# Six buffers of split weights placed at six different addresses modulo 512 bytes

## The chip, the cores and the metric

The kernel runs on one core of one Trainium2 chip. The metric is the device time of one execution in microseconds (us), the median of several runs. Before the change it is 2036.37 us, the median of 3 runs that lie between 2035.35 and 2038.08 us.

## The reference

One decoder layer on 256 tokens with a model width of 2048, all in float32. Cut to what matters:

```python
h = rmsnorm(x, attn_norm_w)
z, xbc, dt_raw, q, k, v, g = split(h @ w_in)          # 2048 -> 20544 columns
y_ssm  = ssd_mixer(z, xbc, dt_raw, ...) @ w_ssm_out    # 4096 -> 2048
y_attn = moba_attention(q, k, v, ...) @ w_attn_out     # 2048 -> 2048
g_ssm, g_attn = split(sigmoid(g + b_gate))
x = x + (g_ssm * y_ssm + g_attn * y_attn) @ w_out      # 2048 -> 2048
h = rmsnorm(x, ffn_norm_w)
u = causal_dwconv(h @ w_up, ffn_conv_w, ffn_conv_b)    # 2048 -> 11264
x = x + (silu(u_gate) * u_up) @ w_down                 # 5632 -> 2048
```

Nearly all arithmetic is in these seven products of a weight matrix with 256 tokens. The attention and the state-space mixer between them are small.

## The kernel before, in words

**Split products.** Every large product is made three times in the fast float32 form ("fp32r") to keep accuracy. A weight w is split into a rounded part `whi` and a remainder `wlo`, the activations likewise into a high and a low part, and a result is the sum of whi·high, whi·low and wlo·high, gathered in one PSUM tile named `mm`.

**The stream of weights.** `unit` (L167) loads 128 x 2048 floats of weights, 1 MB, from HBM into `wraw` (three buffers) by a DMA on SyncE's queue, and makes two chunks of it, c = 0 and 1. For each chunk ScalarE copies 1024 columns into `whi` (L181) and VectorE subtracts to make `wlo` (L182). There are three buffers of `whi` and three of `wlo`, 128 x 1024 floats or 4096 bytes in a partition each, used in turn. So ScalarE can fill a buffer when TensorE has finished the chunk three before.

**Two forms of product.** They differ in which operand sits in the array (the stationary operand, put there by a LDWEIGHTS instruction that the profile counts as PEld) and which is streamed past it (the moving operand).

- `cm_chunk` (L191): the *weights are stationary* and the activations move. For each of 8 blocks of 128 weights of a chunk it issues two matmuls with the same `whi` block (L196 with the high part, L197 with the low part of the activations), then 8 with the blocks of `wlo` (L199). Each moves 256 columns. A chunk is 24 matmuls. This form makes the whole of the kernel from the gates on (about 300 us to the end). The activations are called `hp`, `ot`, `hn`, `yt`, `mt`, `fh` and `a` in turn.
- `tm_chunk` (L340): the *weights move*, 512 columns at a time, and the activations `hp` are stationary (L347 and L348 with `whi`, L353 with `wlo`). This form makes v, q and k, in the first 300 us or so. A chunk is 12 matmuls.

`dt_unit` (L603) uses `whi` alone for a small product, once.

**What sets the order.** The order in which each engine gets its instructions is that of the program text. Steps of the attention and of the mixer are put between units of the weight stream by a small helper (`Spread`). Small matmuls of these steps stand in TensorE's stream between two units: transposes with an identity in `small` (L443, L487 to L489, L701), scores and values of the attention (L209 to L211, operands `kh`, `kl`, `qh`, `ql`, `pth`, `ptl`, `vt`), the mixer's outputs (L752 with 512 columns and L753 with 256, moving `mhl`, stationary `xx`) and a sum over partitions (L264, moving `nsp`, stationary `onesr`).

**Where things lie.** Pools give out SBUF in the order of the program text, and small unused tiles (`pad0` to `pad5`) shift what comes after them. The start addresses in a partition, modulo 512 bytes, in the kernel before:

| tiles | role in matmuls | start modulo 512 |
|---|---|---|
| `hp`, `ot`, `hn`, `yt`, `mt`, `fh`, `a`, `vt` | moving in `cm_chunk`, stationary in `tm_chunk`; `vt` stationary | 0 |
| `whi`, `wlo`, all six buffers | stationary in `cm_chunk`, moving in `tm_chunk` | 64 |
| `mhl` / `xx` | moving / stationary (L752, L753) | 416 / 352 |
| `kh`, `kl` / `qh`, `ql` | moving / stationary (attention) | 416 / 352 |
| `nsp` / `onesr` | moving / stationary (L264) | 352 / 0 |

A block of weights is 128 floats or 512 bytes wide, and a moving operand steps by 1024 or 2048 bytes, so all blocks of a tile have the residue of its start.

Of the kernel before, what the change touches and what calls it, by code (L numbers as in the profile page):

```python
# [8 lines left out]
F32 = mybir.dt.float32  # L9
F32R = mybir.dt.float32r  # L10
# [142 lines left out]
def build(nc, d, out):  # L153
    with tile.TileContext(nc) as tc:
        _body(tc, nc, d, out)


def _body(tc, nc, d, out):
# [3 lines left out]
    base = ctx.enter_context(tc.tile_pool(name="base", bufs=1))  # L162
    dram = ctx.enter_context(tc.tile_pool(name="dram", bufs=1, space=bass.MemoryType.DRAM))
    psum = ctx.enter_context(tc.tile_pool(name="psum", bufs=4, space=bass.MemoryType.PSUM))


    def unit(src, n=2048, before=None):  # L167
        raw = base.tile([128, 2048], F32, name="wraw", bufs=3)
        if before is None:
            nc.sync.dma_start(raw[:, :n], src)  # L170
        parts = []
        for c in range(2):
            hi = base.tile([128, 1024], F32R, name="whi", bufs=3)
            lo = base.tile([128, 1024], F32R, name="wlo", bufs=3)
            m = n // 2 if before is None else n // 4
            for i in range(0, n // 2, m):
                s = slice(c * n // 2 + i, c * n // 2 + i + m)
                if before is not None:
                    nc.sync.dma_start(raw[:, s], src[:, s])
                    before(2 * c + i // m)  # L180
                S.activation(hi[:, i:i + m], raw[:, s], AF.Copy)  # L181
                V.tensor_tensor(lo[:, i:i + m], raw[:, s], hi[:, i:i + m].bitcast(F32), op=SUB)  # L182
            parts.append((hi, lo))
        return parts

    def mm_tile():
        return psum.tile([128, 512], F32, name="mm", bufs=4)
# [13 lines left out]
    def cm_unit(src, xh, xl, nk=16):  # L201
        parts = unit(src, nk * 128)
        ps = mm_tile()[:, :T]
        for c in range(2):
            cm_chunk(ps, parts[c], xh, xl, c * nk // 2, nk // 2, c == 0, c == 1)
        return ps
# [15 lines left out]
    def r32(name):  # L222
        t = base.tile([128, 2, 16, T], F32R, name=name, tag="s32", bufs=3)
        return t, t[:, 0], t[:, 1]

    _, hph, hpl = r32("hp")
# [129 lines left out]
    def tm_units(srcs, after_unit, before=None, mid=None):  # L356
        pst = None
        for u in range(4):
            parts = unit(srcs[u], before=before and (lambda c, u=u: before(4 * u + c)))
            if pst is None:  # L360
                pst = [mm_tile() for _ in range(2)]
            for c in range(2):
                tm_chunk(pst, parts[c], u * 4 + c * 2, u == 0 and c == 0, u == 3 and c == 1)
                if mid and u == 2 and c == 0:
                    mid()
            after_unit(u)
        return pst
# [11 lines left out]
    for cb in range(3):  # L379
        def before(k):  # L380
            if k == 0:
                nc.sync.dma_start(xt[:, 1:3], d["xT"][:, 1:3])
            elif k % 2 == 1 and k < 15:
                nc.sync.dma_start(xt[:, k + 2:min(k + 4, 16)], d["xT"][:, k + 2:min(k + 4, 16)])
            hp_split(k)
# [16 lines left out]
    _, oh_, ol_ = r32("ot")  # L402
# [200 lines left out]
    def dt_unit():  # L603
        raw = base.tile([128, 2048], F32, name="wraw", bufs=3)
        nc.sync.dma_start(raw[:, :1024], d["wdt"])
        rv = raw[:, :1024].rearrange("p (k c) -> p k c", c=64)
        ps = mm_tile()[:, :T]
        for c in range(2):
            w = base.tile([128, 1024], F32R, name="whi", bufs=3).rearrange("p (k a c) -> p k a c", a=2, c=64)
            ks = slice(8 * c, 8 * c + 8)  # L610
            S.activation(w[:, :, 0], rv[:, ks], AF.Copy)
            V.tensor_tensor(w[:, :, 1], rv[:, ks], w[:, :, 0].bitcast(F32), op=SUB)
            for k in range(8):
                wk = w[:, k].rearrange("p a c -> p (a c)")
                PE.matmul(ps, wk, hnh[:, 8 * c + k], start=c == 0 and k == 0, stop=False)
                PE.matmul(ps, wk, hnl[:, 8 * c + k], start=False, stop=c == 1 and k == 7)
        return ps
# [172 lines left out]
    def out_unit(q, u, done):  # L790
        parts = unit(d["wso"][q, u])
        yh, yl = yt[:, q % 2, 0], yt[:, q % 2, 1]
        ps = mm_tile()
        for c in range(2):
            cm_chunk(ps[:, c * T:(c + 1) * T], parts[c], yh, yl, 0, 8, True, True)
        done(u, ps.rearrange("p (a t) -> p a t", t=T))
# [10 lines left out]
    def gate_ssm(o):  # L807
# [3 lines left out]
        if o % 2:  # L811
            nc.gpsimd.dma_start(gs[o // 2], gpair.pop(o // 2))

    dt_steps(dt_unit())
    go = 0
    for step in range(9):
# [20 lines left out]
    _, mh_, ml_ = r32("mt")  # L837
# [23 lines left out]
    _, fh, fl = r32("fh")  # L861
# [101 lines left out]
```

## Time and profile before

| what | value |
|---|---|
| time, median of 3 runs | 2036.37 us |
| the profiled execution's own time | 2037.9 us |
| its span, first to last instruction | 2036.1 us |
| TensorE busy (PE), weight loads (PEld) | 2026.9 us, 1969.9 us |
| VectorE, ScalarE busy | 1478.3 us, 1187.2 us |
| granted TensorE clock | 0.999 |

The page of the profile gives the busy time of each engine, the chain of work that ended last, and the costliest groups of instructions. Matmuls overlap in it, since a matmul is shown from its start to a modelled end (276 ns for one of 256 columns) while the next one starts after about 113 ns. The rate of TensorE is therefore read from the *starts* of matmuls, in the timeline or by counting them in a window, and not from their durations. The timeline merges instructions of one group that follow each other: a row with "x8" starts with the first and ends with the last of eight.

### The profile page before, as it was taken

Reading aid. Unit: us, or ns where it says so; the run is one execution under the profiler, and the core shown is the slowest. Engines: PE = TensorE matmul, PEld = TensorE weight load, DVE = VectorE, ACT = ScalarE, POOL = GpSimd, SP = SyncE. Lnnn points to the kernel's source line nnn. Section 1 sums busy time; section 2 is a strip of 40 time slices with the busy share of each in tenths; the row PEclk is TensorE's granted clock in tenths of the full one; section 3 lists DMA queues with packets and bytes.
Section 4 is the critical chain, followed back from the end, with each engine's and each line's share of the span. In section 5 each row is a group of like instructions: output and inputs, shape, how many; then the busy total and the mean of one; then the engine's idle time right before and its main releaser. Section 6 shows DMA issues by size and latency. Waiting matters only on the chain.

```text
span 2036.1 us, 39538 instructions
## 1 busy us (share of the span) xinstructions
PE 2026.9 (100%) x16539; PEld 1969.9 (97%) x16539; DVE 1478.3 (73%) x2280; ACT 1187.2 (58%) x1678; POOL 43.9 (2%) x84
## 2 busy tenths in 40 slices
PE   9999999999999999999999999999999999999999
PEld 7888889999999999999999999999999999999999
DVE  7567767556698898988988887677777765677554
ACT  6456556444668767666676755565555553455333
POOL 0000000000000000000000010000000000000000
PEclk9999999999999999999999999999999999999999
DMA  7654445655556555555555675555555555555555
GB/s 280 253 183 164 174 160 210 223 200 206 202 196 206 200 202 204 189 190 194 197 190 191 224 286 209 196 188 199 194 188 201 192 191 202 188 194 200 186 184 169
DMA packets 65435, 407.44 MB, mean 200 GB/s; under 512 B 7783, under 2 KB 10152, under 8 KB 21736
## 3 DMA queue, kind: packets, MB, share of 16 engines
q1 hardware_dynamic: 55096, 376.36, 51.6%
q0 software_dynamic: 6560, 22.12, 3.5%
q10 hardware_dynamic: 3600, 6.42, 0.9%
q8 instruction: 129, 2.11, 0.4%
q14 instruction: 50, 0.41, 0.1%
HBM read 398.50 MB, written 9.53 MB: 200 GB/s over the span
## 4 chain that ended last, share of the span: by engine, by line
PE 97%; ACT 1%; DVE 1%; issue 0%; DMA 0%; ACTq 0%; POOLq 0%
PE mm L199 27%; PE mm L196 27%; PE mm L197 27%; PE mm L347 4%; PE mm L353 4%; PE mm L348 4%; PE cc L752 1%; DVE wlo L182 0%; PE cc L209 0%; PE cc L210 0%; PE cc L211 0%; PE cc L753 0%; PE cc L443 0%; ACT whi L181 0%; PE cc L701 0%
## 5 line engine op out<-in xcount | busy, mean ns | idle before, releaser
L181 ACT ACTIVATE whi<-wraw 128x1024 fp32r<-128x1024 f32 (+2 forms) x728 | 756.7, 1041 | 720.6 <-PE mm L197 559.0
L182 DVE TENSOR_TENSOR wlo<-wraw,whi 128x1024 fp32r<-128x1024 f32 (+2 forms) x728 | 870.8, 1198 | 287.8 <-ACT whi L181 281.3
L196 PE MATMUL mm<-hn,whi 128*128 128x256 f32 x1536 | 358.7, 276 | 0.0
L197 PE MATMUL mm<-hn,whi 128*128 128x256 f32 x1536 | 358.4, 276 | 0.0
L197 PE MATMUL mm<-fh,whi 128*128 128x256 f32 x1408 | 327.8, 276 | 0.0
L196 PE MATMUL mm<-fh,whi 128*128 128x256 f32 x1408 | 327.8, 276 | 0.0
L196 PEld LDWEIGHTS mm<-hn,whi 128*128 128x128 f32 x1536 | 288.4, 188 | 1.3
L197 PEld LDWEIGHTS mm<-hn,whi 128*128 128x128 f32 x1536 | 288.4, 188 | 0.1
L197 PEld LDWEIGHTS mm<-fh,whi 128*128 128x128 f32 x1408 | 264.4, 188 | 0.0
L196 PEld LDWEIGHTS mm<-fh,whi 128*128 128x128 f32 x1408 | 264.3, 188 | 0.0
L199 PE MATMUL mm<-hn,wlo 128*128 128x256 f32 x1536 | 205.7, 276 | 0.0
L199 PEld LDWEIGHTS mm<-hn,wlo 128*128 128x128 f32 x1536 | 188.5, 188 | 0.0
L199 PE MATMUL mm<-fh,wlo 128*128 128x256 f32 x1408 | 188.2, 276 | 0.0
L199 PEld LDWEIGHTS mm<-fh,wlo 128*128 128x128 f32 x1408 | 172.7, 188 | 0.0
L196 PE MATMUL mm<-a,whi 128*128 128x256 f32 x704 | 164.3, 276 | 0.0
L197 PE MATMUL mm<-a,whi 128*128 128x256 f32 x704 | 164.3, 276 | 0.0
L347 PE MATMUL mm<-whi,hp 128*128 128x512 f32 x384 | 152.8, 398 | 1.9 <-ACT whi L181 1.7
L348 PE MATMUL mm<-whi,hp 128*128 128x512 f32 x384 | 151.2, 394 | 0.0
L197 PEld LDWEIGHTS mm<-a,whi 128*128 128x128 f32 x704 | 132.2, 188 | 0.0
L196 PEld LDWEIGHTS mm<-a,whi 128*128 128x128 f32 x704 | 132.1, 188 | 0.0
L196 PE MATMUL mm<-yt,whi 128*128 128x256 f32 x512 | 119.5, 276 | 0.0
L197 PE MATMUL mm<-yt,whi 128*128 128x256 f32 x512 | 119.5, 276 | 0.0
(296 smaller groups left out, 3168.2 us busy)
## 6 DMA issues: line engine op xcount, KB each, us to landing
wraw<-wup SPq DMA_DIRECT2D x88, 1024.0 KB, 4.8
wraw<-wssd SPq DMA_DIRECT2D x80, 1024.0 KB, 4.9
wraw<-wqk SPq DMA_DIRECT2D x32, 1024.0 KB, 4.8
wraw<-wso SPq DMA_DIRECT2D x32, 1024.0 KB, 4.8
wraw<-wd SPq DMA_DIRECT2D x32, 1024.0 KB, 4.8
wraw<-wga SPq DMA_DIRECT2D x16, 1024.0 KB, 4.8
wraw<-wao SPq DMA_DIRECT2D x16, 1024.0 KB, 4.9
wraw<-wgs SPq DMA_DIRECT2D x16, 1024.0 KB, 4.8
```

What stands on the lines that cost most here:

```text
L181: S.activation(hi[:, i:i + m], raw[:, s], AF.Copy)
L182: V.tensor_tensor(lo[:, i:i + m], raw[:, s], hi[:, i:i + m].bitcast(F32), op=SUB)
L196: PE.matmul(ps, w, xh[:, k0 + k], start=first and k == 0, stop=False)
L197: PE.matmul(ps, w, xl[:, k0 + k], start=False, stop=False)
L199: PE.matmul(ps, lo[:, k * 128:(k + 1) * 128], xh[:, k0 + k], start=False, stop=last and k == nk - 1)
L347: PE.matmul(pst[tt], hph[:, k0 + k, ts], wh, start=first and k == 0, stop=False)
L348: PE.matmul(pst[tt], hpl[:, k0 + k, ts], wh, start=False, stop=False)
L353: PE.matmul(pst[tt], hph[:, k0 + k, ts], wl, start=False, stop=last and k == 1)
L752: PE.matmul(ps, x0, m[:, :, h * 256:(h + 1) * 256], start=True, stop=False)
```

## The change

Six named tiles with one buffer each take the place of the two rings of three. They are taken in turn by a counter of chunks. A table gives each one a pad ahead of it, a length, and an offset at which it starts, both in floats. Their start addresses modulo 512 become:

| buffer | `whi` 0 | `wlo` 0 | `whi` 1 | `wlo` 1 | `whi` 2 | `wlo` 2 |
|---|---|---|---|---|---|---|
| before | 64 | 64 | 64 | 64 | 64 | 64 |
| after | 64 | 192 | 320 | 320 | 336 | 456 |

The pads and the longer tiles add 512 bytes in all, so every tile that comes after them lies 512 bytes higher with the residue that it had. No engine's instructions change in kind, number or order. The one difference beside the addresses: `dt_unit` now uses up a turn of `wlo` too, so that `whi` and `wlo` of a chunk always have the same number.

```diff
+    homes = [(0, 1024, 0), (32, 1024, 0), (32, 1024, 0), (0, 1024, 0), (0, 1056, 4), (0, 1056, 2)]
+    chunks = [0]
+
+    def chunk_tiles():
+        i = chunks[0] % 3
+        parts = []
+        for j, part in enumerate(("whi", "wlo")):
+            pad, n, at = homes[2 * i + j]
+            if pad and chunks[0] < 3:
+                base.tile([128, pad], F32, name=f"pad_{part}{i}")
+            parts.append(base.tile([128, n], F32R, name=f"{part}_{i}", bufs=1)[:, at:at + 1024])
+        chunks[0] += 1
+        return parts
...
-            hi = base.tile([128, 1024], F32R, name="whi", bufs=3)
-            lo = base.tile([128, 1024], F32R, name="wlo", bufs=3)
+            hi, lo = chunk_tiles()
...
-            w = base.tile([128, 1024], F32R, name="whi", bufs=3).rearrange("p (k a c) -> p k a c", a=2, c=64)
+            w = chunk_tiles()[0].rearrange("p (k a c) -> p k a c", a=2, c=64)
```

## The prediction

> **What bounds the kernel now.** I read the page first: its engine row, the chain that ended last by line, and the waits of TensorE.
>
> ```profile
> PE 2026.9 (100%) x16539; PEld 1969.9 (97%) x16539; DVE 1478.3 (73%) x2280; ACT 1187.2 (58%) x1678; POOL 43.9 (2%) x84
> PEclk9999999999999999999999999999999999999999
> PE 97%; ACT 1%; DVE 1%; issue 0%; DMA 0%; ACTq 0%; POOLq 0%
> PE mm L199 27%; PE mm L196 27%; PE mm L197 27%; PE mm L347 4%; PE mm L353 4%; PE mm L348 4%; PE cc L752 1%; DVE wlo L182 0%; PE cc L209 0%; PE cc L210 0%; PE cc L211 0%; PE cc L753 0%; PE cc L443 0%; ACT whi L181 0%; PE cc L701 0%
> ```
>
> TensorE never stops, its clock is full throughout, and 97% of the chain is matmuls: 81% in the form with stationary weights (L196, L197, L199), 12% in the form with moving weights (L347, L348, L353). The waits of TensorE say how little else there is to win:
>
> ```profile
> PE cc L264 <- DVE nsp L259: 2.6, 3, 0.9
> PE mm L347 <- ACT whi L181: 1.7, 1, 1.7
> PE cc L247 <- DVE onesr L240: 1.1, 1, 1.1
> ```
>
> That is 5.4 us in all. So a change of addresses can move the time in one way only that matters: through the interval from one matmul's start to the next. I read that from the timeline. These are the ends of three chunks of `cm_chunk` in its steady state, and of two in another place:
>
> ```profile
> 1452.15 1.07 PE L199 MATMUL mm<-fh,wlo 128*128 128x256 f32 x8
> ...
> 1476.63 1.07 PE L199 MATMUL mm<-fh,wlo 128*128 128x256 f32 x8
> 1479.36 1.07 PE L199 MATMUL mm<-fh,wlo 128*128 128x256 f32 x8
> ```
>
> ```profile
> 1106.69 1.10 PE L199 MATMUL mm<-yt,wlo 128*128 128x256 f32 x8
> ...
> 1118.00 1.11 PE L199 MATMUL mm<-hn,wlo 128*128 128x256 f32 x8
> ```
>
> From 1452.15 to 1476.63 us lie nine chunks of 24 matmuls: 24.48 / 216 = 113.3 ns each. From 1106.69 to 1118.00 us lie four: 11.31 / 96 = 117.8 ns. Both are the same instructions with the same residues (moving 0, stationary 64), the same clock, no wait. So the interval is not one constant of the instruction. There are two steady rhythms, and what differs can only be how the stream of the moving operand and the weight load that runs under it fall against each other. The row of the first window shows that the fast one is the rule: 100 us hold 100 / 0.1133 = 882 starts, and the 276 ns long matmuls that already run at its left edge make 885.
>
> ```profile
> 430.00:530.00 100.00, 100.00 (x885) 1.00 0.59 209
> 1104.50:1118.50 14.00, 14.00 (x121) 1.00 0.51 184
> 1474.50:1488.50 14.00, 14.00 (x126) 1.00 0.48 173
> ```
>
> **The change part by part: stationary weights.** The number of matmuls comes from the answer on L199:
>
> ```profile
> L199 PE MATMUL mm<-hn,wlo x1536: 276/276/283, 490.1 to 1161.4; 128*128 128x256 f32 x192
> L199 PE MATMUL mm<-fh,wlo x1408: 276/276/278, 1315.9 to 1880.0; 128*128 128x256 f32 x176
> L199 PE MATMUL mm<-a,wlo x704: 276/276/276, 1664.3 to 2032.3; 128*128 128x256 f32 x176
> L199 PE MATMUL mm<-yt,wlo x512: 276/276/283, 765.7 to 1226.9; 128*128 128x256 f32 x171
> L199 PE MATMUL mm<-hp,wlo x256: 276/276/282, 307.4 to 479.1; 128*128 128x256 f32 x128
> L199 PE MATMUL mm<-ot,wlo x256: 276/276/276, 334.1 to 484.5; 128*128 128x256 f32 x128
> L199 PE MATMUL mm<-mt,wlo x256: 276/276/276, 1228.9 to 1314.0; 128*128 128x256 f32 x128
> ```
>
> The sum is 4,928 with `wlo`, and by the code twice as many, 9,856, with `whi`: 14,784. A third falls on each buffer: 3,285 on a `whi`, 1,643 on a `wlo`. Their moving operands keep residue 0. Only the weight load starts elsewhere: unchanged for `whi` 0, at another multiple of 64 bytes for `wlo` 0 (192), `whi` 1 and `wlo` 1 (320), and off every multiple of 64 for `whi` 2 (336 = 5 x 64 + 16) and `wlo` 2 (456 = 7 x 64 + 8).
>
> The trace of before never loads these weights from another residue, so the price must come from its small matmuls. Two places where a chunk of `cm_chunk` is followed by a matmul with another stationary operand, which is loaded under the chunk's last matmul:
>
> ```profile
> 571.00 1.07 PE L199 MATMUL mm<-hn,wlo 128*128 128x256 f32 x8
> 571.91 0.40 PE L752 MATMUL cc<-mhl,xx 128*128 128x512 f32 x1
> 572.15 0.28 PE L753 MATMUL cc<-mhl,xx 128*128 128x256 f32 x1
> 572.27 0.40 PE L752 MATMUL cc<-mhl,xx 128*128 128x512 f32 x1
> 572.50 0.28 PE L753 MATMUL cc<-mhl,xx 128*128 128x256 f32 x1
> 572.62 0.28 PE L196 MATMUL mm<-hn,whi 128*128 128x256 f32 x1
> ```
>
> ```profile
> 612.02 1.07 PE L199 MATMUL mm<-hn,wlo 128*128 128x256 f32 x8
> 612.92 0.39 PE L264 MATMUL cc<-nsp,onesr 128*128 128x512 f32 x1
> ```
>
> Eight intervals take 0.90 us (8 x 113.3 = 907 ns) where the next load starts at residue 0 (`onesr`), a multiple of 64, and 0.91 us where it starts at 352 (`xx`), which is 32 off one. A hundredth is the resolution of the row, so this pair says only that residue 0 costs nothing against 64 and that 352 may cost some ns. What follows is clearer: the four matmuls of `mhl` (416) and `xx` (352) take 0.71 us for 1,536 columns, where six intervals of 113.3 ns would be 0.68. That is 30 ns over, 5 ns for 256 columns. Here both operands lie 32 bytes off a multiple of 64, and the rows don't part the two. For a stationary operand alone that gives the bounds 0 and 5 ns. I take 4.3 ns, near the upper end, because the slow rhythm, 117.8 - 113.3 = 4.5 ns, lies there too and seems to be the state that a bad fall of the two streams leads to.
>
> The bounds below nothing: no 256-column matmul with fp32r weights in this trace has a rhythm below 113.3 ns, whatever its residues. The one quicker rhythm is that of the transposes:
>
> ```profile
> 1118.94 1.04 PE L701 MATMUL cc<-small,pre 128*128 128x128 f32 x8
> ```
>
> ```profile
> L701 PE MATMUL cc<-small,pre 128*128 128x128 f32 x32 | 4.1, 272 | 0.0
> ```
>
> With the last one's 272 ns taken off, seven intervals take 0.77 us, some 109 ns each, but that is another instruction (128 columns of plain float32). So the gain is bounded by 113.3 - 109 = 4.3 ns a matmul and I give it little weight.
>
> The sum for stationary weights: `whi` 1, `wlo` 0, `wlo` 1 at multiples of 64, nothing. `whi` 2 and `wlo` 2: (3,285 + 1,643) x 4.3 ns = 21.2 us.
>
> **Moving weights.** 1,152 matmuls of 512 columns:
>
> ```profile
> L347 PE MATMUL mm<-whi,hp 128*128 128x512 f32 x384 | 152.8, 398 | 1.9 <-ACT whi L181 1.7
> ...
> 160.67 0.39 PE L347 MATMUL mm<-whi,hp 128*128 128x512 f32 x1
> ...
> 163.41 0.39 PE L347 MATMUL mm<-whi,hp 128*128 128x512 f32 x1
> ```
>
> Twelve in 2.74 us are 228 ns each, at moving residue 64 and stationary 0. The nearest row for a moving operand off the multiples of 64 is L752 above (416): 0.24 and 0.23 us, some 235 ns. So `whi` 2 and `wlo` 2, a third or 384 matmuls, cost 0 to 384 x 7 = 2.7 us. I take 1.5 us. The other way, two matmuls of 256 columns at 113.3 make 226.6, so that 1,152 x 2 = 2.3 us is what a better fall of the streams could give.
>
> **The splits.** ScalarE's write and VectorE's subtraction go to the new addresses too:
>
> ```profile
> L182 DVE TENSOR_TENSOR wlo<-wraw,whi 128x1024 fp32r<-128x1024 f32 x680 | 829.5, 1222 | 270.5 <-ACT whi L181 265.6 <-ACT nw L265 3.2
> L181 ACT ACTIVATE whi<-wraw 128x1024 fp32r<-128x1024 f32 x680 | 719.9, 1060 | 680.3 <-PE mm L197 518.7 <-PE mm L348 94.6 <-DVE mhl L742 21.2
> ```
>
> A chunk costs VectorE 1.22 us and ScalarE 1.06 us, TensorE 24 x 113.3 = 2.72 us, and ScalarE idles 518.7 us until L197 frees a buffer. Even a split slowed by 10% (0.12 us) stays under TensorE. In a stage where VectorE has other work for over 1.4 us a chunk this cover is gone; there the same 10% would cost 0.12 us a chunk. I put it at 0. The other turn of `wlo` after `dt_unit` happens once and is hidden likewise.
>
> **The sum**: 21.2 + 1.5 = 22.7 us. On the profiled execution that is 2037.9 + 22.7 = 2060.6. That execution lies 1.5 us above the median, so against the median of 2036.4 I forecast 2059 us, 1.1% slower.
>
> **The rivals.** (1) *Nothing happens.* The fast rhythm is a property of the instruction, the slow one an accident of timing after a wait, and the weight load's address plays no part: 2036 us, with moving weights 2034 to 2040. For it: residue 0 and 64 are alike at 612.92, and 97% or more of all matmuls hold one rhythm while ScalarE, VectorE and the DMAs write the same memory. Against it: two rhythms at one address set show that something is shared. [...] The trace's 117.8 ns beside 113.3 ns, with no wait shown, speaks against it at least in part.
>
> [...]
>
> (3) *The rhythm is lost altogether.* If each switch of buffers with a new residue throws the streams out of the fast rhythm, and it is not found again within a chunk, all but `whi` 0 run at 117.8 or worse: (14,784 - 3,285) x 4.5 = 52 us, and with moving weights 2090 us. For it: once in the slow rhythm, the stretch from 1104 us kept it for 4 chunks until transposes broke it. It decides from the point where recovery takes more than 24 matmuls. Against it: after the four matmuls at 571.91 the fast rhythm is back within one chunk.
>
> (4) *Faster*, the other sign: a weight load that starts further behind the moving operand collides with it less, and the matmul comes near the 109 ns of the transposes. One buffer of `whi` and one of `wlo` at such a residue would give 4,928 x 4.3 = 21 us: 2015 us; moving weights alone 2.3 us. It decides where 113.3 ns is a rhythm that still holds collisions and not a floor. [...]
>
> **How the numbers follow.** My forecast (2048 to 2075 us) gets 0.42, rival 1 0.23, rival 2 0.10, rival 3 and what lies between it and the forecast 0.10, rival 4 0.15. A measurement of this kernel tells 0.2%, some 4 us, from no change. Faster takes rival 4, 0.15; same takes rival 1, 0.23; slower the rest, 0.62. The range reaches from 2032 us (below rival 1) to 2084 us (recovery slow, but not in all buffers); it leaves out most of rival 4 and the full rival 3, less than 2 in 10.
>
> **What would show it.** In the profile of the changed kernel the x8 rows of L199 and the L196/L197 pairs should go by the buffer: chunk after chunk the rows should read 1.07 in two of three and about 1.10 in the third, and three chunks should take 2 x 2.72 + 2.83 = 8.27 us instead of 8.16. Rival 1 shows 1.07 in all, rival 3 about 1.10 in all or most, rival 4 rows under 1.07. The prediction is wrong if the slow rows belong to 192 or 320 as well, if 336 and 456 stay at 1.07, or if the time moves while the rhythm does not, through new waits on L181 or L182.

## The result and the profile after

The changed kernel takes 2066.97 us (median of 4 runs, 2066.93 to 2067.12) against 2035.89 us of the kernel before (median of 4 runs, 2035.35 to 2038.08). The ratio is 1.0148, with a 95% interval of 1.0136 to 1.0159: it is slower by 31.1 us. The forecast was 2059 us within 2032 to 2084.

The page of the profile after, its engine row and the chain by line. All lines of the kernel stand 15 further down, so L199 is now L214, L196 is L211, L347 is L362 and L353 is L368.

```profile
PE 2058.1 (100%) x16539; PEld 2000.0 (97%) x16539; DVE 1479.3 (72%) x2280; ACT 1187.1 (57%) x1678; POOL 43.9 (2%) x84
PE mm L211 27%; PE mm L212 27%; PE mm L214 27%; PE mm L362 4%; PE mm L368 4%; PE mm L363 4%; PE cc L767 1%; ACT whi L196 1%; DVE wlo L197 1%; PE cc L226 0%; PE cc L224 0%; PE cc L225 0%; PE cc L458 0%; PE cc L716 0%; PE cc L768 0%
```

TensorE is busy throughout as before, 31.2 us longer; VectorE and ScalarE are busy for the same time as before to 1 us. TensorE's waits have not grown either (3.4 us, where 5.4 us stood):

```profile
PE cc L279 <- DVE nsp L274: 1.3, 3, 0.5
PE cc L262 <- DVE onesr L255: 1.1, 1, 1.1
PE mm L362 <- ACT whi L196: 1.0, 1, 1.0
```

So the time lies in the interval from one matmul to the next. The timeline of TensorE in the steady state, the `wlo` matmuls that end four chunks, and the first of the chunk that follows:

```profile
1470.85 1.11 PE L214 MATMUL mm<-fh,wlo 128*128 128x256 f32 x8
...
1473.62 1.07 PE L214 MATMUL mm<-fh,wlo 128*128 128x256 f32 x8
...
1476.34 1.07 PE L214 MATMUL mm<-fh,wlo 128*128 128x256 f32 x8
...
1479.15 1.11 PE L214 MATMUL mm<-fh,wlo 128*128 128x256 f32 x8
1480.10 0.28 PE L211 MATMUL mm<-fh,whi 128*128 128x256 f32 x1
1480.21 0.29 PE L212 MATMUL mm<-fh,whi 128*128 128x256 f32 x1
1480.34 0.28 PE L211 MATMUL mm<-fh,whi 128*128 128x256 f32 x1
1480.45 0.28 PE L212 MATMUL mm<-fh,whi 128*128 128x256 f32 x1
1480.57 0.28 PE L211 MATMUL mm<-fh,whi 128*128 128x256 f32 x1
...
1481.93 0.28 PE L214 MATMUL mm<-fh,wlo 128*128 128x256 f32 x1
```

Two chunks in three end in a row of 1.07, as all did before, and the third in one of 1.11: that is `wlo` 2 at 456, whose 8 matmuls take 0.95 us (1479.15 to 1480.10), 119 ns each. From 1476.34 to 1479.15 us lie the 8 of `wlo` 1 at 320, 0.91 us in the fast rhythm, and the 16 of `whi` 2 at 336, which have the other 1.90 us: again 119 ns. The 16 of `whi` 0, from 1480.10 to 1481.93 us, take 1.83 us where 1.81 would be the fast rhythm, although their buffer lies at 64 as it always did. The excess stands in the first four, 0.47 us instead of 0.45. That is the way back from the buffer before.

The difference of starts over the whole trace, by the buffer whose block is loaded, without the few intervals over 300 ns. The last column is measured against 113.46 ns, the mean of the same intervals in the kernel before:

| buffer, start modulo 512 | intervals | mean, ns | over 113.46 ns, us |
|---|---|---|---|
| `whi` 2, 336 | 3,269 | 118.69 | 17.1 |
| `wlo` 2, 456 | 1,635 | 118.31 | 7.9 |
| `whi` 0, 64 | 3,282 | 114.89 | 4.7 |
| `whi` 1, 320 | 3,285 | 113.75 | 1.0 |
| `wlo` 0, 192 and `wlo` 1, 320 | 3,290 | 113.65 | 0.6 |

The sum is 31.3 us. The 1,152 matmuls with moving weights take 268.8 us where they took 269.0 (a sum of a rise and a fall, taken apart further down). The span grew by 29.2 us; the 2 us between are the shorter waits.

The same in one number, which the experiments below repeat: how many matmuls 200 us of the steady state hold (with the two or three that already run at the left edge), before and after:

```profile
1400.00:1600.00 200.00, 200.00 (x1767) 1.00 0.54 195
```

```profile
1400.00:1600.00 200.00, 200.00 (x1736) 1.00 0.52 190
```

200 us by 1,764.6 are 113.3 ns, and by 1,733.6 are 115.4 ns.

### The profile page after: what moved, and what is told of

Its sections match the earlier page's. It is cut to its first block, busy times and chain, and to the rows that moved or that the text cites. A ratio compares the mean times of both kernels' runs of the same rounds, so it can differ in the third digit from the quotient of the medians.

```text
span 2065.3 us, 39538 instructions
## 1 busy us (share of the span) xinstructions
PE 2058.1 (100%) x16539; PEld 2000.0 (97%) x16539; DVE 1479.3 (72%) x2280; ACT 1187.1 (57%) x1678; POOL 43.9 (2%) x84
## 4 chain that ended last, share of the span: by engine, by line
PE 97%; ACT 1%; DVE 1%; issue 0%; DMA 0%; ACTq 0%; POOLq 0%
PE mm L211 27%; PE mm L212 27%; PE mm L214 27%; PE mm L362 4%; PE mm L368 4%; PE mm L363 4%; PE cc L767 1%; ACT whi L196 1%; DVE wlo L197 1%; PE cc L226 0%; PE cc L224 0%; PE cc L225 0%; PE cc L458 0%; PE cc L716 0%; PE cc L768 0%
## 5 line engine op out<-in xcount | busy, mean ns | idle before, releaser
L196 ACT ACTIVATE whi<-wraw 128x1024 fp32r<-128x1024 f32 (+2 forms) x728 | 756.2, 1040 | 753.7 <-PE mm L212 614.5
L211 PE MATMUL mm<-hn,whi 128*128 128x256 f32 x1536 | 365.3, 279 | 0.0
L212 PE MATMUL mm<-hn,whi 128*128 128x256 f32 x1536 | 365.0, 279 | 0.0
L211 PE MATMUL mm<-fh,whi 128*128 128x256 f32 x1408 | 333.5, 278 | 0.0
L212 PE MATMUL mm<-fh,whi 128*128 128x256 f32 x1408 | 333.4, 278 | 0.0
L211 PEld LDWEIGHTS mm<-hn,whi 128*128 128x128 f32 x1536 | 289.0, 188 | 1.2
L211 PEld LDWEIGHTS mm<-fh,whi 128*128 128x128 f32 x1408 | 264.7, 188 | 0.0
L214 PE MATMUL mm<-hn,wlo 128*128 128x256 f32 x1536 | 209.0, 278 | 0.0
L214 PEld LDWEIGHTS mm<-hn,wlo 128*128 128x128 f32 x1536 | 191.3, 188 | 0.0
L214 PE MATMUL mm<-fh,wlo 128*128 128x256 f32 x1408 | 190.7, 278 | 0.0
L214 PEld LDWEIGHTS mm<-fh,wlo 128*128 128x128 f32 x1408 | 174.7, 188 | 0.0
L211 PE MATMUL mm<-a,whi 128*128 128x256 f32 x704 | 167.1, 278 | 0.0
L212 PE MATMUL mm<-a,whi 128*128 128x256 f32 x704 | 167.1, 278 | 0.0
L362 PE MATMUL mm<-whi,hp 128*128 128x512 f32 x384 | 152.5, 397 | 1.1 <-ACT whi L196 1.0
L211 PEld LDWEIGHTS mm<-a,whi 128*128 128x128 f32 x704 | 132.4, 188 | 0.0
L211 PE MATMUL mm<-yt,whi 128*128 128x256 f32 x512 | 121.6, 279 | 0.0
```

Of the source, the lines that this page charges most:

```text
L211: PE.matmul(ps, w, xh[:, k0 + k], start=first and k == 0, stop=False)
L212: PE.matmul(ps, w, xl[:, k0 + k], start=False, stop=False)
L214: PE.matmul(ps, lo[:, k * 128:(k + 1) * 128], xh[:, k0 + k], start=False, stop=last and k == nk - 1)
L362: PE.matmul(pst[tt], hph[:, k0 + k, ts], wh, start=first and k == 0, stop=False)
```

## The experiments

All are the changed kernel with another table of pads, lengths and offsets, in which every tile but the six buffers keeps its residue. Only the two kernels that change `pad0` put the activations (and `ones`, `onesr`, `rb`) at 32 as well, and in `both_plus_32` `wraw` too lies 32 bytes on. Each was timed beside the kernel before. The theory to be tested was that of the prediction: a block of weights that starts off the multiples of 64 bytes is loaded under a matmul at about 118 ns instead of 113.3, and everything else is as it was.

**All six at 64.**

```diff
-    homes = [(0, 1024, 0), (32, 1024, 0), (32, 1024, 0), (0, 1024, 0), (0, 1056, 4), (0, 1056, 2)]
+    homes = [(0, 1024, 0), (0, 1024, 0), (0, 1024, 0), (0, 1024, 0), (0, 1024, 0), (0, 1152, 0)]
```

> Six named tiles as in the changed kernel, but all six at 64 and the 512 bytes given as one pad behind them. If the addresses of the split weights are the whole cause, this gives the time of the kernel before, 2036 us within 0.2%, and 113.3 ns an interval. Rival: the named tiles, the other turn of wlo after dt_unit, or the 512 bytes by which all later tiles moved cost something; then a part of the 31 us stays here and the time is over 2040 us.

2036.55 us, ratio 0.9998 (0.9983 to 1.0012). The addresses are the whole cause; the named tiles, the turn of `wlo` and the 512 bytes cost nothing that can be measured.

**The 16 and 8 bytes taken back.**

```diff
+    homes = [(0, 1024, 0), (32, 1024, 0), (32, 1024, 0), (0, 1024, 0), (0, 1056, 0), (0, 1056, 0)]
```

> Residues 64, 192, 320, 320, 320, 448: only the 16 and 8 bytes of the last two buffers are taken back. My theory (only a start off the multiples of 64 bytes costs) expects 2036 us within 0.2% and the fast interval of 113.3 ns in all six buffers. Rival (any residue other than 64 costs, or the switch between residues does): over 2040 us, with the intervals of 192, 320 and 448 over 114 ns.

2037.35 us, ratio 1.0006 (0.9993 to 1.0019), with this window of its steady state:

```profile
1400.00:1600.00 200.00, 200.00 (x1767) 1.00 0.54 193
```

The 128, 256 and 384 bytes cost nothing that can be measured, the 16 and the 8 cost all. The profiled execution took 2044.5 us, more than the median, because 13% of its intervals fell in the slow rhythm (2% in the profile of before). Single executions of the kernel before reach 2046.8 us too.

**Only one buffer off.**

```diff
+    homes = [..., (0, 1056, 4), (0, 1056, 0)]    # only_336
+    homes = [..., (0, 1056, 0), (0, 1056, 2)]    # only_456
```

> Residues 64, 192, 320, 320, 336, 448: only whi 2 is off. Theory: its 3,280 intervals cost 5.4 ns each as in the changed kernel, 17.6 us, and the first four matmuls of the buffer that follows, which is wlo 2 at 448 here, take some 20 ns more in all to come back to the fast rhythm, 206 times, 4 us: 2057 to 2059 us. Rival (prices are not additive, 336 costs only beside 456): 2036 to 2050 us.

> Residues 64, 192, 320, 320, 320, 456: only wlo 2 is off. Theory: 1,640 intervals at 5.0 ns, 8.2 us, and the return to the fast rhythm in the first four matmuls of whi 0, 4 us: 2048 us. Sum check: this and only_336 together, less the one return that the changed kernel doesn't pay twice, should give the changed kernel's 31 us. [...]

`only_456` came out as expected: 2050.52 us, ratio 1.0065 (1.0050 to 1.0080). Its 456 buffer goes at 119.5 ns, `whi` 0 comes back within four matmuls, and all others are at 113.4 to 113.5 ns. `only_336` did not: 2079.71 us, ratio 1.0211 (1.0196 to 1.0227). With *one* buffer off it is slower than the changed kernel with two: 43.1 us over the kernel before that was timed beside it, where the changed kernel has 31.1 us. The price of the 336 buffer itself is the same (118.7 ns). What is new stands in the aligned buffers behind it. The ends of its chunks in the timeline:

```profile
1483.91 1.07 PE L214 MATMUL mm<-fh,wlo 128*128 128x256 f32 x8
1486.63 1.07 PE L214 MATMUL mm<-fh,wlo 128*128 128x256 f32 x8
1489.44 1.10 PE L214 MATMUL mm<-fh,wlo 128*128 128x256 f32 x8
1492.27 1.10 PE L214 MATMUL mm<-fh,wlo 128*128 128x256 f32 x8
1495.09 1.11 PE L214 MATMUL mm<-fh,wlo 128*128 128x256 f32 x8
1497.94 1.10 PE L214 MATMUL mm<-fh,wlo 128*128 128x256 f32 x8
1500.69 1.07 PE L214 MATMUL mm<-fh,wlo 128*128 128x256 f32 x8
1503.41 1.07 PE L214 MATMUL mm<-fh,wlo 128*128 128x256 f32 x8
1506.23 1.10 PE L214 MATMUL mm<-fh,wlo 128*128 128x256 f32 x8
```

The rows at 1489.44, 1497.94 and 1506.23 us are `wlo` 2 at 448, right behind 336. After 1500 us the two chunks at 64/192 and 320/320 are fast. After 1489 us the *same* two chunks, rows 1492.27 and 1495.09, stay slow to the end, until 336 comes again. Of the intervals of aligned buffers 54% are slow here, 13% in the changed kernel. So the aligned buffers show both rhythms here, and which one they take depends on the buffers before them. Over the whole trace both chunks behind `wlo` 2 end slow in 90 of 208 rounds of three chunks here, and in 14 of 208 in the changed kernel. Behind a 456 buffer four matmuls mostly bring the fast rhythm back; it stands behind 336 in the changed kernel, where 448 stands in `only_336`, and so spared it the worse outcome. What the buffer before leaves behind is not shown by any run. The prices of the two buffers do not add: 43.1 us with 336 alone, 31.1 us with both.

**All six at another residue.** These ask what makes a start good: its own place, or its distance from the moving operand. `both_plus_32` and `moving_32` keep the six in a row without pads.

```diff
+    homes = [(8, 1024, 0), ..., (0, 1144, 0)]      # all_96
+    homes = [(112, 1024, 0), ..., (0, 1040, 0)]    # all_0
+    homes = [(16, 1024, 0), ..., (0, 1136, 0)]     # all_128
+    homes = [(120, 1024, 0), ..., (0, 1032, 0)]    # all_32
-    base.tile([128, 232], F32, name="pad0")        # both_plus_32 and moving_32
+    base.tile([128, 240], F32, name="pad0")
-    base.tile([128, 16], F32, name="pad1")         # moving_32 alone
+    base.tile([128, 8], F32, name="pad1")
```

> All six weight buffers at 96, moving operands still at 0, all later tiles with the residues they had. Theory (a weight block must start at a multiple of 64 bytes): every stationary-weight matmul goes at 117.5 to 119.5 ns, 14,780 x 4.2 to 6.2 ns, so 2098 to 2128 us. Rival (only starts off a multiple of 32 bytes cost, as 336 and 456 are): 2036 us.

> All six weight buffers at 0, the same residue as the moving operands. Theory: 0 is a multiple of 64, so 2036 us within 0.3%. Rival (weight load and moving operand collide when they lie at the same place modulo 64, 128 or 512 bytes, and the 64 bytes between them are what keeps them apart): clearly slower, over 2060 us, since now every load meets the moving stream at the same residue.

> Moving operands at 32 and weights at 96, so that their distance of 64 bytes stays and both starts are off the multiples of 64. Theory (own alignment counts): at least as slow as all_96, 2098 us or more. Rival (the distance between the two counts): 2036 us.

> Moving operands at 32, weights at 64. By the small matmuls of the kernel before, whose moving operands lie off the multiples of 64 and go at 117 to 119 ns, the moving operand's alignment costs like the weights': 2090 to 2120 us, for both forms. Rival (only the weight load's start counts): 2036 us. Here the stationary operands of the first form, hp, lie at 32 too.

> After all_0 (2128 us, 120.0 ns) my rule of the multiples of 64 is not enough: now the distance from the moving operand counts, and 64, 192, 320 and 448 are all 64 modulo 128. New theory (the streams meet again every 128 bytes): weights at 128 with the moving operand at 0 behave as at 0, 120 ns an interval and 2125 to 2131 us. Rival (the streams meet only at the same place modulo 256 or 512, and every other multiple of 64 is good): 2036 us.

> All six weight buffers at 32, moving operands at 0. If only the size of the distance modulo 128 counts and not its sign or whose start is off a multiple of 64, this is like all_96 and moving_32, 118.2 to 118.3 ns and 2105 to 2112 us. If the loss grows towards distance 0, it lies between all_96 (2109 us) and all_0 (2128 us).

| run | moving / stationary start | time, us | ratio (95% interval) | mean interval, ns |
|---|---|---|---|---|
| kernel before | 0 / 64 | 2036 to 2037 | 1 | 113.5 |
| `all_0` | 0 / 0 | 2128.16 | 1.0440 (1.0415 to 1.0466) | 120.0 |
| `all_32` | 0 / 32 | 2110.95 | 1.0359 (1.0343 to 1.0375) | 118.3 |
| `all_96` | 0 / 96 | 2108.76 | 1.0345 (1.0324 to 1.0366) | 118.2 |
| `all_128` | 0 / 128 | 2113.41 | 1.0372 (1.0353 to 1.0391) | 118.7 |
| `moving_32` | 32 / 64 | 2109.28 | 1.0350 (1.0329 to 1.0371) | 118.3 |
| `both_plus_32` | 32 / 96 | 2096.49 | 1.0287 (1.0266 to 1.0307) | 117.6 |

The windows of `all_0`, `all_128` and `both_plus_32`:

```profile
1400.00:1600.00 200.00, 200.00 (x1669) 1.00 0.51 182
```

```profile
1400.00:1600.00 200.00, 200.00 (x1687) 1.00 0.51 185
```

```profile
1400.00:1600.00 200.00, 200.00 (x1700) 1.00 0.52 186
```

`all_96` did as the theory said, but `all_0` and `all_128` ended it: both start at a multiple of 64 and are among the slowest. The expectation for `all_128` after that, that it would be like `all_0`, failed as well: it is slow, but at 118.7 and not 120.0 ns, so a start at 128 is not one at 0 over again. `moving_32` came out as expected. `all_32` is like `all_96` within 2.2 us; its time lies in the ranges of both of its cases, so it doesn't part them. The pairs with a fast rhythm as the rule in these runs all have both starts on multiples of 64 and a distance of 64 modulo 128 (64, 192, 320 and 448 beside 0; 113.3 ns in the window of `multiples_of_64`, which holds as many matmuls as that of the kernel before). `both_plus_32` has that distance with both starts off the multiples: its interval is the slow rhythm of the kernel before (117.6 beside 117.8 ns), with about 520 of its 14,761 intervals at 113 or 114 ns (128 in `all_96`, 19 or fewer in the other four slow runs). Its time lies just under the 2098 us of its theory and far from the rival's 2036 us: the distance alone doesn't give the fast rhythm. Nor is the distance told from the weights' own place, since a moving operand at another multiple of 64 than 0 was not run.

ScalarE and VectorE write the weights at the new addresses too, so their writes could have been what slows TensorE. The trace of `all_0` speaks against that: the 474 intervals in which neither of them ran have a mean of 120.0 ns, as have the 7,750 in which both ran.

**A version that might beat both.** In `all_0` the matmuls with *moving* weights were quicker, 227.3 ns in the mean where the kernel before has 229.5. The ends of its chunks beside those of the kernel before:

```profile
160.46 1.07 PE L368 MATMUL mm<-wlo,hp 128*128 128x512 f32 x4
163.18 1.07 PE L368 MATMUL mm<-wlo,hp 128*128 128x512 f32 x4
```

```profile
162.50 1.08 PE L353 MATMUL mm<-wlo,hp 128*128 128x512 f32 x4
165.25 1.08 PE L353 MATMUL mm<-wlo,hp 128*128 128x512 f32 x4
```

That is 2.72 us for 12, against 2.75. So two kernels give each chunk another place in its buffer when the weights move (`moving` is true in `tm_units`) than when they stand:

```diff
+    homes = [(0, 1040, 0), (0, 1040, 0), (0, 1040, 0), (0, 1040, 0), (0, 1040, 0), (0, 1072, 0)]
+            at = 16 * (moving != (j == 1))                        # moving_0_stationary_64
+    homes = [(32, 1040, 0), (0, 1040, 0), (32, 1040, 0), (0, 1040, 0), (0, 1024, 0), (0, 1024, 0)]
+            at = 16 * (moving != (j == 1)) if i < 2 else 0        # moving_0_of_256
```

> Every buffer is 64 bytes longer, and a unit starts its chunk at one of two places in it: 64 modulo 128 where the weights are stationary, 0 modulo 128 where they move. all_0 had its moving-weight matmuls at 226.9 ns where the kernel before has 229 to 230. Theory: both forms get their better distance, so 1,152 x 2.6 ns = 3 us less than the kernel before, 2033 to 2034 us. Rival (the gain of the first form in all_0 came with its slower second form, or the 128 bytes between buffers bring it into the slow rhythm): 2036 us or more.

> In moving_0_stationary_64 the moving-weight matmuls went at 227 to 229 ns from residue 256 but at 232 to 234 ns from 128 and 384, so the two streams meet modulo 256, not 128. Here four of the six buffers let the weights move from 0 modulo 256 and stand at 64 modulo 128; the last two stay at 64 for both. Theory: 227 to 227.5 ns in the four, 229 to 230 ns in the two, 113.3 to 113.7 ns in the stationary form: 768 x 2.5 ns = 2 us less than the kernel before, 2034.5 to 2035.5 us. Rival (128 or 256 bytes play no part, the gain in all_0 had to do with its other form): 229 ns or more in all six and 2037 us or more.

Neither beats the kernel before: 2039.74 us, ratio 1.0010 (1.0000 to 1.0021), and 2039.46 us, ratio 1.0007 (0.9998 to 1.0017). In the second, the moving weights at 0 do go at 227.0 to 227.6 ns, but those at 256 at 228.2 to 230.6, so in this ring 256 does not do what 0 does, and all 1,152 together save 0.4 us. The stationary form takes 2.5 us more, because 6% of its intervals are slow where 2% were. Its six buffers stand at 192, 320, 448, 64, 64 and 64. Whether changing between good residues lets the slow rhythm in more often is not shown: `multiples_of_64` changes between them too, and its median can't be told from that of the kernel before.

## Why the prediction was right, and where it was not

- *TensorE's interval is the only place where addresses can move the time.* Shown: `all_64_new_tiles` gives the time back, the busy times of the other engines are unchanged to 1 us, TensorE's waits are 2 us shorter and not longer, and the intervals hold 31.3 us.
- *`whi` 2 and `wlo` 2 cost 4.3 ns an interval, 21.2 us.* The place is right, the term was too small: 5.2 and 4.9 ns, 25.0 us. The upper bound of 5 ns from `mhl` and `xx` was the better value, though not a bound: 336 goes over it.
- *The other four buffers cost nothing.* For their own addresses this holds (`multiples_of_64`). But 4.7 us went to `whi` 0, whose address never changed, and 1.6 us to the other three. The sum lacked a term for what a buffer leaves to the next one. Rival 3 named that effect and set its turning point at 24 matmuls; the changed kernel mostly needs four and passes the point in 14 of 208 rounds, `only_336` in 90 of 208. That the omission cost only 6.3 us here is luck of the layout: with 448 in the place of 456 (`only_336`) the aligned buffers cost 27.6 us.
- *Moving weights cost 1.5 us.* The size was right, the place only in part. The 1,118 intervals that are under 300 ns in both profiles took 1.4 us longer in all: 0.8 us in `whi` 2 and `wlo` 2, but 0.5 us in `wlo` 0, whose 192 is a multiple of 64 and was put at nothing. The total of 268.8 us after 269.0 hides this, because in the profile of before the granted clock was half for some 3.4 us near the start, and six of these matmuls took 426 or 427 ns there. That stretch in the profile of before and the same place in the one after (the clock is the last number but two):

```profile
7.90:11.40 3.50, 3.37 (x9) 0.51 1.04 393
```

```profile
7.50:11.00 3.50, 3.39 (x15) 1.00 1.04 356
```

- *The splits are hidden.* Yes: VectorE 1479.3 us after 1478.3, ScalarE 1187.1 after 1187.2.
- *The sign to look for* came as it was described: x8 rows of 1.07, 1.07 and 1.11, and three chunks in 8.30 us (1470.85 to 1479.15), where 1.10 and 8.27 us were named. Rows of 192 and 320 are slow too in the 14 rounds above.
- *A start at a multiple of 64 is good.* The step from the one row with `onesr` at 0 failed as a rule. That pair of rows shows a single load at residue 0 that costs nothing, and `all_0` shows that a stream of such loads goes at 120.0 ns. One load at that place did not tell the rhythm that a stream of them settles to.
- *Rivals 1 and 2.* By rival 1 the address of the weight load plays no part. Here the interval went from 113.5 to 120.0 ns by the address of the stationary operand alone (`all_0`), and with both operands moved by 32 bytes (`both_plus_32`, 117.6 ns) it is shorter than with either one alone (`all_96` 118.2, `moving_32` 118.3). So the address plays a part, and the two starts act together. By rival 2 only the start at 456 costs. The start at 336 goes at 118.7 ns and holds 17.1 of the 31.3 us, and `only_336`, without a start at 456, is 43.1 us slower than the kernel before.

Why one pair of starts is fast and another slow is not shown by any run. That the price hangs on both starts together is shown by the three runs with 32 bytes more (117.6 to 118.3 ns), and that it hangs on the buffers that came before by the share of slow intervals in aligned buffers, 54% in `only_336` and 13% in the changed kernel.

## What to carry to other kernels

Where TensorE loads new weights under every matmul, place the stationary and the moving operand deliberately, here the moving one at 0 and the stationary one at 64 modulo 128 (a mean interval of 113.5 ns in the kernel before, of 117.6 to 120.0 ns in the six runs with another pair for the whole ring), and keep every buffer of a ring there: with one buffer at 336, 54% of the intervals of the aligned buffers were slow as well. Judge a layout by the starts of matmuls over a long steady stretch and not by one load or one buffer: in these runs a buffer's rhythm depended on the one before it, and the prices of two buffers did not add.

## What the runs showed of the hardware that was not expected

- The same matmul with the same addresses went in two stable rhythms, 113.3 and 117.8 ns, and kept either for chunks on end (1104 to 1119 us in the profile of before; 90 of 208 rounds of `only_336`).
- Equal starts (`all_0`) are the worst place found in these runs for the stationary form (120.0 ns) and the best one found for the moving form (227.3 ns for 512 columns).
- A start at 128 did not repeat what 0 did: 118.7 beside 120.0 ns in the stationary form, 232.4 beside 227.3 ns in the moving form (`all_128` and `all_0`).
